# A hybrid attention/SSD layer: TensorE's first phase put into program order, with the SSD blocks cut into two stages and the norms moved

## The chip, the core and the metric

The kernel runs on one core of a Trainium2 chip. The metric is the device time of one execution in microseconds (us), as the median of several runs; less is better. TensorE (PE in the profile) does the matmuls and the transposes and writes to PSUM; PEld is its weight load. VectorE (DVE), ScalarE (ACT) and GpSimd (POOL) work on the results, and SyncE (SP) issues the DMAs.

## What is computed

One layer of a streaming encoder over 2048 prompt tokens and 32 sample tokens, width 1024. The part that the change touches is the input projection and the SSD (Mamba-2) half of the mixer; the stick-breaking attention of the first token block runs beside it.

```python
h = rmsnorm(x, g_mix_pre)
proj = h @ w_in                     # q, k, v (512 each), z (512), xbc (768), dt (8)
xbc = silu(causal_conv4(xbc)); xh, bm, cm = split(xbc)
dt = softplus(dt_raw + dt_bias); a = -exp(a_log)
acum = cumsum(dt * a)               # in chunks
y = ((cm @ bm.T) * tril(exp(acum_t - acum_s))) @ (dt * xh)    # within a chunk
y += (cm * exp(acum)) @ h_in                                   # from the state before it
h_out = exp(acum_end) * h_in + (bm * exp(acum_end - acum) * dt).T @ xh
y = rmsnorm((y + d_skip * xh) * silu(z), g_ssm_out)
attn = stick_breaking(q, k, v)      # past keys and values come from a cache for the sample tokens
out = concat([rmsnorm(attn, g_attn_out), y]) @ w_out
# then residual, gated conv FFN, residual
```

## The kernel before

Tokens lie in four blocks (`SBS`): block 0 has 512 prompt and the 32 sample tokens, blocks 1 to 3 have 512 each. The kernel has a first phase (`phase_in`), which makes all projections and the SSD part of the four blocks, and then a tail in which the attention of block s+1 is interleaved with the output projection and the FFN of block s.

**Products.** A product is a 128-column piece of `w_in` times the block's tokens: `dense` (L118) issues three fp32r matmuls for each of eight 128-row pieces (weights and activations are split into a high and a low part), so 24 matmuls of 512 columns in blocks 1 to 3, and two tiles of 24 matmuls of 272 columns in block 0. All of them have line L126. A block has 22 products: six for the convolution (`wbx`, of which numbers 4 and 5 are B and C), four each for k, v, z and q. A product leaves PSUM from one of two banks named `o`, multiplied by `r`, the broadcast reciprocal root of the input norm (`kf` L293, or `t` L305 in the convolution). `weight` makes a weight's two parts: a DMA, a cast on ACT (L110) and a subtraction on POOL (L111); three weights are held.

**Block of tokens s, in the order in which the program writes it.** `take` splits x into `xhi` (ACT L262) and `xlo` (DVE L263); for block 0 it also sums the squares (POOL L242) and makes `r`. Then the six convolution products with their convolution and SiLU; the `dt` product (L333 to L336) and its chain of small operations (L344 to L387); then the SSD sub-blocks of 128 tokens (five in block 0, four in the others), each followed by one k product; the squares of the next block's x (`ahead`); four v products, each followed by transposes into a PSUM bank named `st` and a copy on ACT (L427, L429); four z products (the gate) with the sums of squares; the gated norm's `rstd_narrow`; four q products; and last the normed y, stored by DMA.

**An SSD sub-block** (`ssd_block`, L469) loads `acB` and `eA`, the broadcast cumulative sums, by DMA (L478, L484), subtracts and exponentiates (DVE L488, ACT L492, L493), multiplies C by B and by the state into PSUM bank `y` (L498, L500), masks (DVE L506), multiplies into `acB` (L510) and `eA` (L514), transposes x and B (L521, L532) and makes `xdt`, `xw` and `bT` from them (L523, L528, L534), does the products with `acB` (L538), and updates the state (L550 to L562). `st` is one PSUM bank, `y` another tile with one buffer; each of the tiles of `sd` (`acB`, `eA`, `xdt`, `xw`, `bT`) has one buffer.

**The norms' roots** (`rstd_steps`) are matmuls against ones into `st` (L154), two small DVE operations, a power on POOL (L172), and matmuls that broadcast the result, again into `st` (L183), which ACT copies out.

**Who sets the order.** The instruction order of every engine, TensorE too, is set at compile time by a list scheduler that runs a timeline of its own: of the instructions that it takes to be ready it picks the one written first. `pin` and `mark` add order edges between matmuls; before the change the first phase has them only in the attention's slots, and the products there are not pinned. In the tail all products are pinned.

**Early attention.** `early` is a generator: first the sample tokens' attention (`sample`), then the 32 slots of block 0's attention (`slots(0, 0)`: scores L769 and L773, weights L619 to L627, transposes L790, values L805). `build` advances it by `RATE` = 0.66 of a step after each of `phase_in`'s yields, from block 1 on.

```python
            for n in phase_in(kn, c2):
                debt += n
                while debt >= 1:
                    debt -= 1
                    next(early, None)
            for _ in early:
                pass
```

## Time and profile before

| | us |
|---|---|
| median of 3 runs | 3098.43 (3097.11 to 3099.04) |
| the profiled execution | 3091.8 |
| its span, first to last instruction | 3090.0 |
| PE busy / DVE busy / POOL busy / ACT busy in the span | 2881.3 / 1616.4 / 1297.2 / 1278.7 |
| mean granted TensorE clock | 0.970 of full speed |

The first phase ends in the profile at about 858 us, where the first operation of the tail (ACT L713) starts. A row of the windows view gives a stretch of time, its length, the busy time of PE, PEld, DVE, ACT and POOL with the number of instructions, then the granted TensorE clock, the DMA engines' share and GB/s. A row of the waits view gives who waited for which writer, the time in total, how often, and the longest. A row of the groups gives line, engine, operation, shapes and count, then busy time and the mean of one in ns, then idle time before them and what ended it. Busy times of a group count overlapping instructions once.

### The profile page before, as it was taken

How to read it: one execution, taken by the hardware profiler on the slowest of the kernel's cores; microseconds unless marked ns; L12 is line 12 of the kernel's file. 1: busy time of each engine (PE TensorE's matmuls, PEld its weight loads, DVE VectorE, ACT ScalarE, POOL GpSimd, SP SyncE). 2: the span in 40 equal slices, each digit the busy share in tenths (PEclk: the TensorE clock that was granted, in tenths of full speed). 3: DMA queues.
4: the chain of work that ended last, by engine and by line, in shares of the span. 5: the costliest groups of instructions: out<-in, count | busy, mean ns of one | idle time of the engine just before them, and what ended most of it. 6: DMA issues, size and time to landing. Idle time of an engine off the chain costs nothing.

```text
span 3090.0 us, 43496 instructions
## 1 busy us (share of the span) xinstructions
PE 2881.3 (93%) x16142; PEld 2340.0 (76%) x16142; DVE 1616.4 (52%) x2456; ACT 1278.7 (41%) x2511; POOL 1297.2 (42%) x1099
## 2 busy tenths in 40 slices
PE   7899899898898999999999999999999999999996
PEld 6786576676686989998767777785677778878885
DVE  5647757676537565433763434447544453443334
ACT  4325446644457654333653323347333343421211
POOL 4445456464456555554652222246322223521113
PEclk8989999899999999999999999999999999999998
DMA  3536755655574767776646554664554545665555
GB/s 101 179 116 214 249 178 182 195 171 154 164 278 150 234 213 254 234 263 244 220 151 201 179 176 164 208 228 151 192 175 159 178 167 205 191 211 197 176 195 175
DMA packets 242437, 592.57 MB, mean 192 GB/s; under 512 B 49514, under 2 KB 105650, under 8 KB 212658
## 3 DMA queue, kind: packets, MB, share of 16 engines
q1 hardware_dynamic: 242226, 589.78, 57.9%
q8 instruction: 129, 2.11, 0.3%
q14 instruction: 82, 0.67, 0.1%
HBM read 456.19 MB, written 133.50 MB: 191 GB/s over the span
## 4 chain that ended last, share of the span: by engine, by line
PE 67%; DVE 12%; DMA 7%; issue 5%; ACT 4%; POOL 4%; SPq 1%; DVEq 0%; POOLq 0%; ACTq 0%
PE o L126 37%; PE t L126 9%; PE u L126 9%; PE pa L805 4%; PE z L769 3%; PE pt L790 3%; DVE prow L622 2%; DMA acB<-acD 1%; DVE xcA L312 1%; POOL w L111 1%; DVE acB L488 1%; DMA xr<-xT 1%; DVE f L1040 1%; DMA t<-xT 1%; ACT w L110 1%
## 5 line engine op out<-in xcount | busy, mean ns | idle before, releaser
L126 PE MATMUL o<-xhi,w 128*128 128x512 f32 (+2 forms) x4640 | 1202.2, 343 | 33.4 <-DVE kf L293 11.1
L126 PEld LDWEIGHTS o<-xhi,w 128*128 128x128 f32 x4640 | 810.9, 192 | 146.6 <-DVE kf L293 12.6
L126 PE MATMUL o<-xlo,w 128*128 128x272 f32 (+2 forms) x2320 | 794.9, 343 | 13.5 <-DVE xlo L263 7.2
L111 POOL TENSOR_TENSOR w<-wraw,w 128x1024 fp32r<-128x1024 f32 (+2 forms) x172 | 396.7, 2307 | 291.1 <-ACT w L110 266.3
L126 PEld LDWEIGHTS o<-xlo,w 128*128 128x128 f32 x2320 | 444.3, 192 | 67.1 <-DVE xlo L263 9.5
L627 POOL TENSOR_TENSOR beta<-beta,prow 128x512 f32<-128x512 f32 (+4 forms) x264 | 265.3, 1006 | 449.8 <-DVE prow L622 409.8
L126 PE MATMUL o<-ah,w 128*128 128x272 f32 (+1 forms) x1344 | 362.0, 344 | 10.6 <-DVE f L1019 6.7
L972 POOL TENSOR_TENSOR y<-y,gb 128x512 f32<-128x512 f32 (+1 forms) x88 | 115.7, 1315 | 530.7 <-ACT gb L971 530.2
L622 DVE TENSOR_TENSOR_SCAN prow<-gam,prow,z 128x513 f32<-128x513 f32 x200 | 254.7, 1276 | 122.5 <-ACT beta L620 117.0
L126 PE MATMUL u<-xhi,w 128*128 128x512 f32 (+1 forms) x1056 | 300.9, 362 | 0.6 <-ACT r L189 0.5
L126 PEld LDWEIGHTS o<-ah,w 128*128 128x128 f32 x1344 | 235.7, 189 | 42.1 <-DVE f L1019 8.5
L110 ACT CAST w<-wraw 128x1024 fp32r<-128x1024 f32 (+2 forms) x172 | 171.3, 997 | 168.7 <-PE o L126 123.1
L619 ACT ACTIVATE gam<-z 128x512 f32<-128x512 f32 (+3 forms) x330 | 178.6, 542 | 131.0 <-PE z L769 77.5
L126 PE MATMUL o<-al,w 128*128 128x272 f32 (+1 forms) x672 | 227.3, 338 | 0.0
L126 PEld LDWEIGHTS u<-xhi,w 128*128 128x128 f32 x1056 | 189.0, 188 | 38.5 <-issue 4.0
L964 DVE SCALAR_TENSOR_TENSOR y<-gb,cv,y 128x512 f32<-128x512 f32 (+1 forms) x176 | 167.2, 951 | 81.6 <-ACT y L962 78.5
L793 ACT COPY wt<-pt 128x512 f32<-128x512 f32 (+3 forms) x282 | 147.8, 533 | 136.9 <-PE pt L790 135.3
L126 PE MATMUL u<-xlo,w 128*128 128x512 f32 (+1 forms) x528 | 190.3, 360 | 0.0
L790 PE MATMUL pt<-ident,beta 128*128 128x128 f32 x1088 | 177.7, 280 | 8.6 <-POOL beta L627 6.0
L790 PEld LDWEIGHTS pt<-ident,beta 128*128 128x128 f32 x1088 | 131.5, 143 | 63.1 <-issue 22.6
L620 ACT ACTIVATE beta<-z 128x512 f32<-128x512 f32 (+3 forms) x330 | 178.6, 541 | 0.0
L1019 DVE TENSOR_TENSOR f<-o,f 128x272 f32<-128x272 f32 (+1 forms) x208 | 114.0, 550 | 114.3 <-PE o L126 112.2
(253 smaller groups left out, 4452.3 us busy)
## 6 DMA issues: line engine op xcount, KB each, us to landing
w<-wS_up SPq DMA_DIRECT2D x132, 1024.0 KB, 5.0
w<-wS_dn SPq DMA_DIRECT2D x72, 768.0 KB, 4.7
w<-wS_out SPq DMA_DIRECT2D x47, 1024.0 KB, 6.2
wS_up<-w SPq DMA_DIRECT2D x44, 1024.0 KB, 4.8
wraw<-wup SPq DMA_DIRECT2D x44, 512.0 KB, 5.7
k<-kS SPq DMA_DIRECT2D x80, 256.0 KB, 4.0
wS_dn<-w SPq DMA_DIRECT2D x24, 768.0 KB, 4.4
w<-wS_dn SPq DMA_DIRECT2D x32, 512.0 KB, 4.2
```

The source lines that it names most:

```text
L110: nc.scalar.copy(hi[:, :n, :], raw[:, :n, :])
L111: nc.gpsimd.tensor_tensor(lo[:, :n, :], raw[:, :n, :], hi[:, :n, :].bitcast(F32), op=ALU.subtract)
L126: mm = nc.tensor.matmul(ps[:, : c1 - c0], l[:, k, :], at(r, k0 + k)[:, c0:c1], start=first and i == 0 and k == 0, stop=last and i == 2 and ...
L619: nc.scalar.activation(g[:, c0:512], z, AF.Sigmoid, scale=-0.125)
L620: nc.scalar.activation(b[:, :n], z, AF.Sigmoid, scale=0.125)
L622: nc.vector.tensor_tensor_scan(back(pr), back(g), z[:, 0:1].to_broadcast([P, n + 1]), self.kn.ones[:, 0:1] if prev is None else prev, op0= ...
L627: eng.tensor_tensor(b[:, :n], b[:, :n], pr[:, c0 + 1 : 513], op=ALU.mult)
L790: mm = nc.tensor.transpose(t[:, P * j : P * j + P], w[:, P * j : P * j + P], kn.ident[:])
L793: copy(wt[:, : n // P, P * b : P * b + P], t[:, :n].rearrange("p (i q) -> p i q", q=P))
L805: nc.tensor.matmul(av[DH * (j % 2) : DH * (j % 2) + DH, c0:], v[:, j, :], wt[:, j, c0:], start=kc == s and j < 2, stop=kc == 0 and j > 1,)
L964: nc.vector.scalar_tensor_tensor(y[:, :W], gb[:, i : i + W], kn.col(wc + i), y[:, :W], op0=ALU.mult, op1=ALU.add)
L972: nc.gpsimd.tensor_tensor(y[:, :W], y[:, :W], t, op=ALU.mult)
```

## The change

All matmuls and transposes are issued through a small class, `Ordered`. In the first phase it is strict: each one is pinned behind the one before, so TensorE runs the first phase in the order in which the program writes it. The program is rewritten to fit this.

Work is laid on 23 units to each block of tokens, which are 22 products and the `dt` product. `after(n, fn)` puts a function off by n units, and `todo` lists what is done after a unit. Blocks 1 to 3 take the `dt` product first, then convolution, k, v, q, and z last; block 0 takes `dt` as the fourth unit.

- The first three convolution products of block 0 leave PSUM by a plain ACT copy (`bare`); the factor `r`, the convolution and the SiLU follow when `r` is there. `r`'s two steps come after the second and the third unit.
- The chain behind `dt` is cut into four steps, after units 1, 4, 6 (block 0: 4, 7, 8).
- `ssd_block` becomes a generator with three parts: the loads and exponentials; a first stage with the transposes and the products of C; a second stage with the products with `acB` and the state. The stages come after units 8, 9, 10, 12, 13, 15, 16, 18 (block 0: 9 to 18). The loads of a sub-block follow the second stage of the one before it.
- The transposes of B go into the bank of `y`; the state's matmuls go ahead of the products with `acB`; the four DVE operations of L542 move to the first stage.
- The transposes of v come two units after their product. The next block's squares are spread over units 9 to 12, its `r` over the next two.
- The gated norm's two steps come three and four units after the last z product, which is in the next block of tokens; the normed y follows there.
- In `sample` the products with the values come one step later, and two yields are added at its end (12 yields where there were 10).

```diff
+class Ordered:
+    def __init__(self, kn):
+        self.kn, self.strict = kn, False
...
+    def put(self, mm):
+        if self.strict:
+            self.kn.pin(mm)
+            self.kn.mark(mm)
+        return mm
...
+    def root(s, sq, first, second, done=None):
+        r = rp.tile([P, 544], F32, name=f"r{s % 2}")
+        g = kn.rstd_steps(rp, psm, "st", [sq], SBS[s][1], D, out=r)
+        after(first, lambda: next(g))
+        after(second, lambda: (next(g), done and done()))
+        return r
+
+    def after(units, fn):
+        pend.append([units, fn])
+
+    def tick():
+        for p in pend:
+            p[0] -= 1
+        due = [p for p in pend if p[0] <= 0]
+        pend[:] = [p for p in pend if p[0] > 0]
+        for p in due:
+            p[1]()
...
+            bare = s == 0 and c in (4, 5, 0)
...
+                    if bare:
+                        nc.scalar.copy(raw[:, d0:d1], ps[:, p0:p1])
+                    else:
+                        nc.vector.tensor_tensor(raw[:, d0:d1], ps[:, p0:p1], r[:, c0 + p0 : c0 + p1], op=ALU.mult)
...
+        def block(b, stage):
+            def go():
+                next(small["blocks"][b], None)
+                if stage == 1 and b < nb - 1:
+                    next(small["blocks"][b + 1])
...
+            after(2, turn)
...
+            if c == 3:
+                rg = rp.tile([P, 544], F32, name=f"r{s % 2}")
+                g = kn.rstd_steps(rp, psm, "st", [small["sq"]], nt, 512, out=rg)
+                after(3, lambda: next(g))
+                after(4, lambda end=normed: (next(g), end(rg, xcA)))
...
+        dt_at = 3 if s == 0 else 0
+        units = cs[:dt_at] + [lambda: next(st)] + cs[dt_at:] + k + v + q + z
+        todo = {i: [lambda: next(st)] for i in ((4, 7, 8) if s == 0 else (1, 4, 6))}
+        for n, i in enumerate(range(9, 19) if s == 0 else (8, 9, 10, 12, 13, 15, 16, 18)):
+            todo.setdefault(i, []).append(block(n // 2, n % 2))
+        if not last:
+            for i in range(4):
+                todo.setdefault(9 + i, []).append(lambda i=i: ahead(i))
...
+            r = root(0, sq0, 2, 3, begin)
+        for i, unit in enumerate(units):
+            unit()
+            tick()
+            for f in todo.get(i, ()):
+                f()
+            yield 0.0 if s == 0 else RATE
+    while pend:
+        tick()
...
     nc.scalar.activation(eA[:, :, :q], eA[:, :, :q], AF.Exp)
+    yield
     h_in = hT[state["h"]] if hS is None else hS
+    ps = psm.tile([P, 512], F32, name="st")
+    for j in range(4):
+        kn.pe.transpose(ps[:q, j * P : j * P + P], xcA[:, j, sl], kn.ident[:])
     cy = psy.tile([P, 2, 512], F32, name="y")
+    kn.pe.transpose(cy[:q, 0, 3 * P : 4 * P], xcB[:, 0, sl], kn.ident[:])
...
+    for j in range(4):
+        nc.vector.scalar_tensor_tensor(
+            xcA[:, j, sl], xcA[:, j, sl], kn.col(C_DS + j), eA[:, j, :q], op0=ALU.mult, op1=ALU.add
+        )
+    yield
     ps = psm.tile([P, 512], F32, name="st")
+    for g in range(2):
+        kn.pe.matmul(
+            ps[g * 64 : g * 64 + 64, :256], bT[:q, g * 64 : g * 64 + 64],
+            xw[:q, 4 * g : 4 * g + 4, :].rearrange("p h d -> p (h d)"), start=True, stop=True,
+        )
     yt = psy.tile([P, 2, 512], F32, name="y")
...
+            kn.pe.strict = True
             early = chain(att.sample(c2), att.slots(0, 0))
...
             out = att.out
+            kn.pe.strict = False
```

More of the change, by code (lines that the diff above doesn't have):

```diff
@@ L266, in take @@
             )
-            if r is None:
+            if s == 0:
                 square(sq, x, k == 0)
-        return (xhi, xlo), r or root(s, sq)
+        return (xhi, xlo), sq
     wfirst = kn.weight(wp, a["wbx"][4])
@@ L294, in leave, with conv @@
             return dst
[L296 to L298 removed]
+        def conv(c):
             raw = tmp.tile([P, 550], F32, name="t")
@@ L330, in phase_in @@
-        for c0, c1 in tiles_of(nt):
-            ps = psd.tile([P, 512], F32, name="o")
-            for k in range(KC):
-                nc.tensor.matmul(
-                    ps[:16, : c1 - c0], wdt[:, k, :], xhi[k][:, c0:c1], start=k == 0, stop=False, skip_group_check=True
-                )
-                nc.tensor.matmul(
-                    ps[:8, : c1 - c0], wdt[:, k, 0:8], xlo[k][:, c0:c1], start=False, stop=k == KC - 1,
-                    skip_group_check=True,
-                )
-            nc.vector.tensor_tensor(dtr[:16, c0:c1], ps[:16, : c1 - c0], r[:16, c0:c1], op=ALU.mult)
@@ L444, in phase_in, with gate @@
+        def gate(c):
+            z = leave(a["wz"][c])
+            xcA = xc["A"]
             t = tmp.tile([P, 550], F32, name="t")
@@ new lines, in ahead @@
+        def ahead(i):
+            nonlocal nxt
+            if i == 0:
+                small["sqn"] = tmp.tile([P, 544], F32, name="sq", bufs=1)
+            for k in (2 * i, 2 * i + 1):
+                square(small["sqn"], load(s + 1, k), k == 0)
+            if i == 3:
+                nxt = root(s + 1, small["sqn"], 1, 2)
+        q, k, v, z = (
+            [(lambda c=c, f=f: f(c)) for c in range(4)]
+            for f in (lambda c: keys("wq", kn.qS, c), lambda c: keys("wk", kn.kS, c), val, gate)
+        )
@@ L647, in sample, with values @@
         av = self.pa.tile([P, 512], F32, name="pa", bufs=1)
-        prev = [None, None]
+        prev, late = [None, None], []
+        def values():
+            for kc, g, q, nsub, wt, v in late:
+                for i in range(nsub):
+                    for e in range(2):
+                        kn.pe.matmul(
+                            av[DH * e : DH * e + DH, P * g : P * g + P], wt[:q, P * i + DH * e : P * i + DH * e + DH],
+                            v[:q, i, P * e : P * e + P],
+                            start=kc == 4 and g == 0, stop=kc == 0 and g == 1 and i == 3, skip_group_check=True,
+                        )
+            late.clear()
         for kc in (4, 3, 2, 1, 0):
```

430 lines of the change are left out of this document (224 added, 206 removed).

## The prediction

> **What bounds the kernel now.** I read the page first.
>
> ```profile
> span 3090.0 us, 43496 instructions
> PE 2881.3 (93%) x16142; PEld 2340.0 (76%) x16142; DVE 1616.4 (52%) x2456; ACT 1278.7 (41%) x2511; POOL 1297.2 (42%) x1099
> ```
>
> PE is busy for 93% of the span and no other engine for more than 52%, so PE's path sets the time, and a change can win only where PE is idle or its clock is held down. The windows view, cut at the starts of the four token blocks and at the end of the first phase (858 us), says where that is.
>
> ```profile
> 0.00:40.00 40.00, 17.78 (x80) 15.98 (x81) 19.71 (x28) 17.52 (x28) 24.44 (x30) 0.74 0.41 142
> 40.00:236.00 196.00, 172.79 (x1290) 161.46 (x1289) 107.34 (x229) 65.74 (x106) 80.25 (x48) 0.90 0.43 132
> 236.00:450.00 214.00, 190.50 (x987) 139.06 (x985) 144.15 (x215) 100.89 (x155) 113.46 (x67) 0.95 0.65 209
> 450.00:655.00 205.00, 185.00 (x902) 138.02 (x901) 143.22 (x211) 117.30 (x188) 113.23 (x77) 0.93 0.61 191
> 655.00:858.00 203.00, 180.42 (x876) 133.66 (x877) 128.70 (x204) 93.82 (x157) 98.49 (x67) 0.95 0.54 171
> 858.00:3090.00 2232.00, 2134.80 (x12018) 1751.84 (x12014) 1073.27 (x1573) 883.45 (x1882) 867.37 (x811) 0.99 0.59 198
> ```
>
> In the first phase PE is busy for 746.5 of 858 us, which leaves 111.5 us idle, at a clock of 0.74 to 0.95. The tail, whose products are pinned, is busy for 2134.8 of 2232 us (96%) at 0.99. So more than half of PE's whole idle time of 208.7 us lies in 28% of the span, and it is the part that the change rewrites. Next, the same view for the stretches in which the small slices dip, and one without a dip for comparison.
>
> ```profile
> 24.00:37.00 13.00, 4.51 (x20) 3.96 (x20) 0.45 (x3) 1.63 (x2) 6.17 (x5) 0.50 0.19 68
> 100.00:120.00 20.00, 14.77 (x100) 13.08 (x99) 13.57 (x24) 5.54 (x8) 12.16 (x9) 0.83 0.68 218
> 140.00:180.00 40.00, 29.23 (x182) 24.96 (x183) 19.34 (x61) 7.19 (x13) 5.41 (x4) 0.66 0.30 90
> 285.00:400.00 115.00, 94.11 (x550) 66.35 (x550) 78.64 (x140) 58.07 (x84) 58.07 (x38) 0.91 0.71 236
> 485.00:600.00 115.00, 98.22 (x507) 70.50 (x506) 82.70 (x150) 74.78 (x114) 61.95 (x45) 0.90 0.66 207
> 680.00:790.00 110.00, 94.84 (x470) 67.73 (x468) 77.09 (x148) 51.63 (x79) 44.14 (x27) 0.91 0.44 137
> 400.00:440.00 40.00, 39.98 (x180) 32.47 (x181) 20.03 (x24) 13.32 (x19) 22.18 (x13) 1.00 0.45 132
> ```
>
> And the windows view of the products alone (L126):
>
> ```profile
> 180.00:230.00 50.00, 47.70 (x369) 1.00 0.45 134
> 370.00:400.00 30.00, 2.90 (x13) 0.77 0.58 193
> 580.00:600.00 20.00, 0.00 (x0) 0.66 0.45 143
> 770.00:790.00 20.00, 0.00 (x0) 0.74 0.38 120
> 400.00:440.00 40.00, 38.94 (x163) 1.00 0.45 132
> ```
>
> The pattern is the same in every token block. While SSD sub-blocks run, products are used up as filler, and at the end of the SSD stretch none is left: 370 to 400, 580 to 600 and 770 to 790 hold 2.9 us of products in 70 us. Small matmuls then wait for one another there, and the clock drops to 0.66 to 0.77. After it the remaining products run back to back at full clock. The waits view of PE in 0 to 860 us names the waits:
>
> ```profile
> PE y L538 <- DVE acB L510: 12.2, 10, 2.4
> PE o L126 <- DVE kf L293: 11.1, 6, 5.2
> PE z L769 <- DVE prow L622: 10.7, 12, 2.0
> PE o L126 <- DVE xlo L263: 7.2, 5, 4.4
> PE o L126 <- ACT xhi L262: 6.9, 1, 6.9
> PE st L154 <- POOL sq L242: 6.2, 1, 6.2
> PE st L550 <- ACT bT L534: 5.7, 4, 2.2
> ...
> PE st L183 <- ACT r L181: 0.7, 1, 0.7
> ```
>
> These are many short waits of a chain on itself (the longest 6.9 us), not one late engine.
>
> **The change part by part.** It adds and removes hardly any work on PE. What it moves is when products stand between the links of the chains. I take each stretch's idle time and its clock loss as what can be won, and then a share. Clock loss is bounded by busy time times (1 minus the clock): at most that if all of it is limited by the array, nothing if it is waiting time.
>
> *The start (bare copies).* The timeline of PE:
>
> ```profile
> 23.73 0.43 PE L126 MATMUL o<-xhi,w 128*128 128x272 f32 x1
> 30.41 2.06 PE L154 MATMUL st<-ones,sq 128*128 128x1 f32 x10 [6.25 <-POOL sq L242]
> ...
> 37.26 0.59 PE L126 MATMUL o<-xhi,w 128*128 128x272 f32 x1
> ```
>
> The first product ends at 24.2 us and fills both `o` banks, which cannot be emptied before `r` exists, so the next product starts at 37.26. With plain copies out, two products fit there: 48 matmuls at 47.70/369 = 0.129 us are 6.2 us each. Their weights are there in time: by POOL's timeline the third weight of the phase ends at 22.3:
>
> ```profile
> 19.41 2.84 POOL L111 TENSOR_TENSOR w<-wraw,w 128x1024 fp32r<-128x1024 f32 x1
> ```
>
> The root's matmuls (4.51 us at half clock) are still to be done, about half of that at full clock: 13 - 2.3 = 10.7, taken as **-11**. The 13.7 us idle in the first 40 us outside this stretch are x arriving and being split; they stay.
>
> *The `dt` chain and the SSD of block 0* (100 to 120 and 140 to 180). Idle 5.2 + 10.8 = 16.0; clock at most 14.77 x 0.17 + 29.23 x 0.34 = 12.4; together 28.4. The chain's steps now have a product or more between them. The tight place is a sub-block's loads, which go out behind the second stage of the one before, two products (12.4 us) ahead of its own second stage. These rows are of DVE's waits and groups:
>
> ```profile
> DVE acB L488 <- DMA acB<-acD: 40.2, 12, 7.3
> ```
>
> ```profile
> L488 DVE TENSOR_SCALAR acB<-acB,acum 128x128 f32<-128x128 f32 (+1 forms) x136 | 43.0, 387 | 40.4 <-DMA acB<-acD 40.2
> L446 DVE TENSOR_TENSOR t<-kf,t 128x512 f32<-128x512 f32 (+1 forms) x16 | 37.7, 2359 | 19.6 <-ACT t L445 19.6
> L510 DVE TENSOR_TENSOR acB<-acB,cbm 128x512 f32<-128x512 f32 (+1 forms) x34 | 30.1, 925 | 6.8 <-ACT acB L492 6.8
> ```
>
> Load at its longest 7.3, eight L488 at 0.387 are 3.1, two L510 at 0.925 are 1.9: 12.3 us before the exponential is counted. That is no margin, so I take three quarters: **-21**.
>
> *The SSD stretches of blocks 1 to 3.* Idle 20.9 + 16.8 + 15.2 = 52.9; clock at most 94.11 x 0.09 + 98.22 x 0.10 + 94.84 x 0.09 = 26.8; together 79.7. Here three products lie between a load and its second stage, 3 x 24 x 38.94/163 us = 17.2 against the 12.3, and first and second stage stand one or two products (5.7 or 11.5 us) apart. DVE is busy for 0.68 to 0.72 of these stretches, so it can keep up but will at times be late with emptying an `o` bank (the 11.1 us of kf waits). I take 0.7: **-56**. The bounds are 0 and 79.7.
>
> How much of it is clock? The row of 580 to 600 has a clock of 0.66, and the longest PE wait listed between 578 and 602 is 2.2 us:
>
> ```profile
> PE st L550 <- ACT bT L534: 2.2, 1, 2.2
> ```
>
> So here the clock fell without a long gap, in a stretch of small matmuls only, and products set between them should hold it at 1.00 as in 400 to 440. The Trainium skill, TensorE: Matmul & The Clock Gate, section "HAM oscillation — how this bites in real kernels", gives the abstract rule of no PE-idle gaps above about 3.4 us; this stretch disagrees with it as the sole condition. By that rule no wait that I expect behind the change would cost clock, and the 39.2 us of clock bounds above would come back whole instead of at three quarters and 0.7: about 11 us more.
>
> *New: `st` changes hands with nothing between.* In program order a v transpose, a root step and a stage of a sub-block follow one another after units 12 to 15, all through the one bank `st`, and PE, now strictly in order, stands until ACT or DVE has emptied it; behind it the next product waits. By the lists I count six such places in block 0, five each in blocks 1 and 2, three in block 3: 19. The nearest row is the same kind of handover, L183 behind ACT's copy, 0.7 us; the upper is the bT wait, 5.7/4 = 1.4. 13 to 27; I take the nearest: **+13**.
>
> *New: z is last.* In blocks 0 to 2 the gated norm's first matmuls come a product and the `dt` product later, which covers the chain. After block 3 nothing is left but the end of the early attention, so PE stands for the gate's chain, in which L446 alone is 2.4 us; q's products did cover that. Between nothing and twice to three times this: **+5**. The same order takes q's stores off the end, off PE's path.
>
> *At nothing:* more exponential/sigmoid alternation on ACT and three more DVE operations, under 144 of 214 us DVE busy at most; the moved DMAs on SP, as long as three weights are ahead.
>
> Sum: -11 - 21 - 56 + 13 + 5 = **-70 us**. The profiled execution took 3091.8 us with a span of 3090.0, which would become 3020; the median of the runs is 3098.43 (3097.11 to 3099.04), so the forecast is **3028 us**.
>
> **The rivals.**
>
> *All of it comes back.* The stages are far enough apart, nothing waits and the clock stays at 1.00: -11 - 28 - 80 + 9 for handovers and end (half of the 18) is -110, 2988 us. For it: 400 to 440 and the pinned tail. Against it: DVE at 0.7. The clock rule cited above would work this way. Chance 0.17.
>
> *Waits move.* Each of the 34 stages waits as the bT reader does now, 1.4 us: 48 us, so -22, 3076 us. For it: PE can no longer take a product while a link is late, and an attention step (z behind prow, 12 waits now) sits in the same line. Against it: the spacing. Chance 0.15, of which 0.04 is no change.
>
> *Slower.* The loads of `acB` sit in SP's queue behind stores and weights that wait, and every second stage waits for them; in order, nothing can pass. At the longest load wait of today, 7.3 us, 17 sub-blocks give +124 and with the -70 a time of 3152. It decides from 70/17 = 4.1 us each. For it: this is DVE's second largest wait (40.2 us). Against it: today it is paid with one product between sub-blocks, not two or three. Chance 0.12.
>
> That the order is not really changed I leave out: the pins reach every matmul of the phase.
>
> **How the numbers follow.** Forecast, -35 to -95 us: 0.56. A measurement tells about 0.2% (6 us) from no change. Faster by more: 0.56 + 0.17 + 0.11 = 0.84; within: 0.04; slower: 0.12. The range is 2980 to 3095: it leaves out the slower case, the no-change part and the far end of the full gain, 0.2 in all.
>
> **What would show it.** Right: the first phase ends near 788 us; products start again right behind 24 us; clock 0.97 or more from 50 us on; no stretch of 20 us without products; L538 and L550 almost gone from PE's waits; `st` readers behind ACT copies with about 20 waits of 0.7 us. Wrong: PE waits of over 3 us at L538 behind acB, DVE above 0.85 in the SSD stretches, or waits of L126 behind L293 grown past 11 us. The tail should be the same to within a few us; a gain or a loss there would be a cause that I have not seen.

## The result and the profile after

| | before | after |
|---|---|---|
| median of 4 runs, us | 3097.77 (3094.78 to 3099.04) | 3136.05 (3130.27 to 3141.71) |
| the profiled execution's span, us | 3090.0 | 3133.6 |
| its granted TensorE clock | 0.970 | 0.962 |
| end of the last projection product, us | 839.8 | 859.1 |
| PE idle up to there, us | 106.5 | 137.1 |

The change makes the kernel slower: ratio 1.0125, 95% interval [1.0105, 1.0145], 38 us. The forecast was 70 us faster. (Of the four runs of f5_noload, further down, one took 4339.69 us at a granted clock of 0.591 for 0.976 to 0.979 in the others; its ratio is of those three.)

The first two lines of the page after:

```profile
span 3133.6 us, 43470 instructions
...
PE 2888.5 (92%) x16142; PEld 2352.5 (75%) x16142; DVE 1612.0 (51%) x2453; ACT 1297.6 (41%) x2534; POOL 1300.4 (41%) x1099
```

The work is the same; PE is busy for 7 us more and idle for 36 us more. Where the idle time lies is read from the windows view. First each kernel from its start to the end of its last projection product; before:

```profile
0.00:839.80 839.80, 733.26 (x4055) 579.79 (x4056) 532.70 (x869) 382.42 (x601) 416.61 (x274) 0.92 0.55 172
```

and after:

```profile
0.00:859.10 859.10, 722.03 (x4017) 577.13 (x4018) 517.45 (x858) 398.20 (x617) 417.24 (x271) 0.92 0.54 169
```

PE's idle time is the second number less the third: 106.5 and 137.1 us. The clock over the whole stretch is the same 0.92 (a better start makes up for 0.92 instead of 0.94 from 50 us on), so it is mainly idle time that was added. Of the 43.6 us by which the span grew, 19.3 are there by the last product, 10.9 lie between it and the 100th matmul of the tail's products, and 13.4 in the rest of the tail.

Now the stretches of the prediction, after:

```profile
24.00:37.00 13.00, 12.92 (x85) 12.89 (x85) 1.32 (x3) 3.75 (x9) 4.96 (x3) 0.79 0.15 51
...
140.00:180.00 40.00, 31.34 (x231) 28.69 (x228) 13.71 (x43) 8.90 (x14) 7.87 (x5) 0.88 0.35 112
285.00:400.00 115.00, 98.09 (x551) 73.14 (x551) 65.58 (x101) 59.80 (x84) 63.53 (x37) 0.94 0.77 254
485.00:600.00 115.00, 94.26 (x449) 71.52 (x448) 75.87 (x121) 68.05 (x101) 64.59 (x41) 0.90 0.66 215
680.00:790.00 110.00, 89.56 (x442) 70.50 (x440) 73.82 (x126) 53.49 (x83) 50.77 (x30) 0.91 0.50 155
```

And products alone (L71 into `o`, which includes the `dt` product):

```profile
580.00:600.00 20.00, 11.26 (x43) 0.91 0.76 239
770.00:790.00 20.00, 9.49 (x40) 0.93 0.50 158
```

The change does what it says. The start is filled (4.51 us busy became 12.92), products now stand in the stretches that had none, and there the clock is 0.91 to 0.93 where it was 0.66 to 0.74 (370 to 400, with 12.79 us of products for 2.90, has 0.89 for 0.77). But the SSD stretches as wholes are hardly fuller: 98.09 for 94.11, 94.26 for 98.22, 89.56 for 94.84. The gaps are now between the products instead of behind them. PE's waits in 0 to 890 us, after:

```profile
PE o L71 <- DVE xlo L293: 19.8, 12, 6.8
PE st L71 <- ACT khi L474: 17.7, 8, 5.7
PE o L71 <- ACT xhi L292: 14.4, 4, 6.5
PE st L74 <- DVE xcA L363: 13.4, 2, 7.9
PE z L71 <- DVE prow L735: 13.0, 6, 6.2
PE pa L71 <- ACT wt L803: 11.1, 4, 4.1
PE st L74 <- ACT khi L474: 10.6, 5, 3.3
PE st L71 <- ACT klo L483: 7.3, 3, 6.5
...
PE st L71 <- ACT r L201: 5.9, 2, 4.8
...
PE st L71 <- POOL sq L519: 4.6, 1, 4.6
PE y L71 <- DVE acB L637: 4.1, 1, 4.1
PE st L74 <- ACT r L209: 2.8, 3, 1.5
```

The waits that were the aim are gone: of the wait for L510's `acB` (12.2 us, ten times) one is left, L637, and the wait for `bT` is not listed. Longer ones came: for the copies of v's transposes out of `st` (khi, klo), for the roots' copies (r), for the last convolution's SiLU (xcA L363), for the early attention's own steps (prow, wt), and for x (xhi, xlo): 17.7 of these 34.2 us are block 0's x at the start, 16.5 the next block's x at a block's end.

What is late behind a 6 us wait? PE's timeline in block 0, then ACT's in the same stretch (start, duration, engine, line, operation, and in brackets the idle time before and who ended it):

```profile
130.69 0.60 PE L74 MATMUL st<-ident,kf 128*128 128x128 f32 x4
132.51 0.29 PE L74 MATMUL st<-ident,kf 128*32 128x128 f32 x1 [1.23 <-ACT khi L474]
139.33 1.12 PE L71 MATMUL st<-xw,bT 128*64 128x256 f32 x4 [6.53 <-ACT klo L483]
```

```profile
131.88 0.58 ACT L474 COPY khi<-st 128x512 f32<-128x512 f32 x1
138.41 0.63 ACT L604 ACTIVATE eA<-eA 128x512 f32<-128x512 f32 x1 [5.95 <-DMA eA<-acD]
138.94 0.24 ACT L483 COPY klo<-st 32x128 f32<-32x128 f32 x1
```

PE put a transpose into `st` at 132.51 and needs the bank back for the state's matmuls. The copy that empties it takes 0.24 us, but in ACT's queue it stands behind the exponential on `eA`, and ACT stood 5.95 us there for a DMA. SP issued that load at 134.62, since `eA` has one buffer, and its last reader (L647) had ended at 134.59:

```profile
134.62 1.29 SPq L595 DMA_DIRECT2D eA<-acD  x2
```

So PE stands for ACT, and ACT for a load; each runs its instructions in the order set for it.

This is the longest of the waits for khi and klo, and not all are of its kind. Eleven of them are over 1 us, 32.8 us together. In five (16.3 us) an exponential on `eA` or `acB` is one of the two instructions just ahead of the copy in ACT's queue; in the other six the one just ahead is a cast, of a weight (L130) or of k or q (L492).

### The profile page after: what moved, and what is told of

It reads as the page before. It is cut to its first block, busy times and chain, and to the rows that moved or that the text cites. A ratio compares the mean times of both kernels' runs of the same rounds, so it can differ in the third digit from the quotient of the medians.

```text
span 3133.6 us, 43470 instructions
## 1 busy us (share of the span) xinstructions
PE 2888.5 (92%) x16142; PEld 2352.5 (75%) x16142; DVE 1612.0 (51%) x2453; ACT 1297.6 (41%) x2534; POOL 1300.4 (41%) x1099
## 4 chain that ended last, share of the span: by engine, by line
PE 71%; DVE 8%; DMA 6%; ACT 4%; issue 3%; POOL 2%; SPq 1%; ACTq 0%; DVEq 0%; POOLq 0%
PE o L71 40%; PE u L71 9%; PE t L71 9%; PE pa L71 4%; PE z L71 4%; PE pt L74 3%; DVE prow L735 2%; DMA xr<-xT 1%; PE y L71 1%; DMA eA<-acD 1%; DMA xr<-hS 1%; ACT w L130 1%; DMA acB<-acD 1%; DVE f L1166 1%; PE st L71 1%
## 5 line engine op out<-in xcount | busy, mean ns | idle before, releaser
L71 PE MATMUL o<-xhi,w 128*128 128x512 f32 (+2 forms) x4640 | 1209.8, 344 | 27.8 <-ACT xhi L292 6.5
L71 PEld LDWEIGHTS o<-xhi,w 128*128 128x128 f32 x4640 | 818.3, 193 | 142.5 <-issue 13.4
L71 PE MATMUL o<-xlo,w 128*128 128x272 f32 (+2 forms) x2320 | 796.0, 343 | 18.8 <-DVE xlo L293 11.2
L71 PEld LDWEIGHTS o<-xlo,w 128*128 128x128 f32 x2320 | 447.5, 193 | 67.9 <-DVE xlo L293 12.6
L71 PE MATMUL o<-ah,w 128*128 128x272 f32 (+1 forms) x1344 | 362.5, 345 | 9.8 <-DVE f L1145 7.3
L71 PE MATMUL u<-xhi,w 128*128 128x512 f32 (+1 forms) x1056 | 300.8, 362 | 0.6 <-ACT r L209 0.5
L130 ACT CAST w<-wraw 128x1024 fp32r<-128x1024 f32 (+2 forms) x172 | 171.3, 996 | 252.1 <-PE o L71 185.3
L71 PEld LDWEIGHTS o<-ah,w 128*128 128x128 f32 x1344 | 236.4, 189 | 41.4 <-DVE f L1145 9.9
L71 PE MATMUL o<-al,w 128*128 128x272 f32 (+1 forms) x672 | 227.9, 339 | 0.0
L71 PEld LDWEIGHTS u<-xhi,w 128*128 128x128 f32 x1056 | 188.9, 188 | 38.5 <-issue 4.0
L71 PE MATMUL u<-xlo,w 128*128 128x512 f32 (+1 forms) x528 | 190.3, 360 | 0.0
L74 PE MATMUL pt<-ident,beta 128*128 128x128 f32 (+1 forms) x1122 | 183.4, 281 | 4.8 <-POOL beta L740 3.6
L74 PEld LDWEIGHTS pt<-ident,beta 128*128 128x128 f32 (+1 forms) x1122 | 135.3, 143 | 60.3 <-issue 26.0
```

The source lines that it names most:

```text
L71: return self.put(self.kn.nc.tensor.matmul(*args, **kw))
L74: return self.put(self.kn.nc.tensor.transpose(*args, **kw))
L130: nc.scalar.copy(hi[:, :n, :], raw[:, :n, :])
```

## The experiments

The reading of the trace gave this theory: program order on PE is itself the cost, since PE then inherits every late place in ACT's and DVE's queues; among these the loads of `acB` and `eA` are the largest, and the block's edges are the next. The rivals: the one bank `st`; the lateness of one engine (ACT); the new places themselves, whatever the order. All ratios are to the kernel before, timed beside each kernel on the same chip; brackets are 95% intervals. Differences from the changed kernel are differences of ratios times 3098 us, a few us off from the differences of the medians. Idle is PE's idle time up to the last projection product, from rows as above. The last two columns are of one profiled execution each: f1_zq's and f4_zqeexp's are the longest of their four, p4_attfree's and q1_eexp's the shortest.

| kernel | median, us | ratio | last product, us | PE idle to there, us |
|---|---|---|---|---|
| before | 3097.77 | 1 | 839.8 | 106.5 |
| after | 3136.05 | 1.0125 [1.0105, 1.0145] | 859.1 | 137.1 |
| x1_free | 3077.95 | 0.9937 [0.9922, 0.9952] | 807.0 | 88.9 |
| x2_oldpin | 3271.34 | 1.0567 [1.0549, 1.0584] | 993.6 | 241.4 |
| x3_vbank | 3133.48 | 1.0122 [1.0102, 1.0141] | 854.2 | 139.6 |
| x4_end | 3129.01 | 1.0105 [1.0082, 1.0128] | 858.0 | 136.2 |
| p1_rate | 3142.85 | 1.0156 [1.0131, 1.0180] | 877.5 | 143.8 |
| p2_vfree | 3138.40 | 1.0132 [1.0106, 1.0158] | 864.8 | 142.0 |
| p3_zq | 3117.22 | 1.0076 [1.0045, 1.0106] | 856.5 | 134.2 |
| p4_attfree | 3116.76 | 1.0068 [1.0046, 1.0091] | 842.6 | 120.7 |
| q1_eexp | 3123.66 | 1.0078 [1.0054, 1.0103] | 843.8 | 129.3 |
| q2_vdve | 3133.33 | 1.0112 [1.0082, 1.0142] | 854.8 | 133.2 |
| r1_noload | 3104.63 | 1.0017 [1.0004, 1.0030] | 831.9 | 121.5 |
| r2_sum | 3103.61 | 1.0019 [1.0006, 1.0033] | 832.8 | 117.0 |
| f1_zq | 3058.47 | 0.9870 [0.9850, 0.9890] | 792.4 | 77.9 |
| f4_zqeexp | 3065.16 | 0.9898 [0.9878, 0.9918] | 798.1 | 81.6 |
| f5_noload | 3048.18 | 0.9822 [0.9792, 0.9852] | 780.9 | 76.9 |

### The order, with and without the new places

x1_free keeps every new place and takes the pins away:

```diff
-            kn.pe.strict = True
+            kn.pe.strict = False
```

> The changed program with the strict order of TensorE switched off in the first phase, so that the scheduler again chooses the order; spacing, z last and everything else as changed. Theory A (TensorE in order stands behind late releases, above all of the one bank st: 52.8 us of its 144.8 us of waits in the changed first phase): 3070 to 3105 us, 30 to 65 us under the changed kernel's 3136, and the waits of st readers behind ACT copies fall from 52.8 us to under 20. Rival B (the moves cost, not the pinning: z last and dt first at a block's edge, the late start, the end): 3125 us or more, with the same waits at the edges.

x2_oldpin is the kernel before, untouched but for the class `Ordered` and `strict = True` over its first phase: the pins without the new places.

> The kernel before with one thing added: all matmuls and transposes of the first phase pinned in program order; no step is moved. Theory A: much slower than before, since each SSD sub-block's chain then stands on TensorE's path with one product between: by 17 sub-blocks at 8 to 12 us each, 3230 to 3300 us. Rival B: pinning costs little, under 3130 us.

The four combinations are: old places free 3098, old places pinned 3271, new places free 3078, new places pinned 3136. The pins cost 173 us on the old places and 58 on the new. The new places are worth 20 us without pins and 135 with them. PE's waits of x1_free:

```profile
PE z L71 <- DVE prow L735: 15.6, 11, 3.2
PE o L71 <- DVE xlo L293: 9.9, 4, 6.7
PE o L71 <- ACT xhi L292: 9.4, 3, 6.7
PE o L71 <- DVE t L343: 8.6, 3, 4.4
```

No `st` reader is among the first; those behind ACT's copies, 44.6 us in the changed kernel (the expectation's 52.8 counts other readers of `st` too), are down to 4.3. The waits for x at the blocks' ends fell from 16.5 to 4.4 us: the scheduler has put other matmuls ahead of what is late. And of the old places with pins:

```profile
PE st L74 <- DVE xdt L543: 40.9, 17, 7.7
PE y L71 <- DVE acB L530: 38.3, 28, 7.0
```

Here the chain of every sub-block shows on PE (17 times `xdt`, 28 times `acB`). The new places do take these away; they were made for the pins, and make good most of what the pins cost.

### The bank, and the engine that empties it

x3_vbank puts v's transposes into the attention's bank `pt`:

```diff
-                ps = psm.tile([P, 512], F32, name="st")
+                ps = kn.ptv.tile([P, 512], F32, name="pt")
```

> The changed kernel with the transposes of v written to the early attention's bank pt instead of st. Theory A: the 36 us of waits behind the copies of v (khi, klo) shrink to 10 to 15, some come back as waits for pt; 3105 to 3122 us, 14 to 30 us under the changed kernel. Rival B: within 6 us of 3136.

The ratio is that of the changed kernel. The wait changed its bank and kept its releaser:

```profile
PE pt L74 <- ACT khi L474: 28.9, 8, 8.1
```

Not the bank, then: the copy of khi is late wherever it copies from. p2_vfree leaves only v's transposes out of the strict order:

```diff
             def turn(s=s):
+                kn.pe.strict = False
...
+                kn.pe.strict = True
```

> The changed kernel with only the transposes of v taken out of the strict order; everything else stays pinned. Theory A (a pinned TensorE stands in front of the next reader of st until ACT has copied v out): 3100 to 3116 us, and the waits of st behind khi and klo fall from 35.9 us to under 12. Rival B (ACT is late anyway, so the stages of the SSD behind them wait for the same copy wherever the transposes stand): 3125 or more.

No gain, as the rival said: the stage behind waits for the same copies (khi 14.0 and 10.5 us, klo 8.0). q2_vdve moves the copies from ACT to DVE:

```diff
-                nc.scalar.copy(vt[:, :512], ps[:])
+                nc.vector.tensor_copy(vt[:, :512], ps[:])
```

> The changed kernel with the copies of v's transposes out of PSUM on VectorE in place of ScalarE; order as in the changed kernel. Theory (they are late since ScalarE stands ahead of them): TensorE's waits for v's copies (khi 17.7 and klo 7.3 us, and 10.6 us of transposes behind them) fall to a third and the time is 3112 to 3128. Rival (VectorE's queue is as late at these places, behind the normed rows and the SSD's multiplies): 3130 or more.

3133.33, 1.0112 [1.0082, 1.0142]: no difference that can be told from the changed kernel. The waits for khi are nearly as long, behind the other engine (klo's 7.3 us fell to 1.3):

```profile
PE st L71 <- DVE khi L474: 16.7, 8, 4.9
...
PE st L74 <- DVE khi L474: 10.9, 5, 5.2
```

The theory that ACT alone is late fell here. One thing that DVE stands for itself is `acB`'s load; in the changed kernel and then in q2_vdve:

```profile
DVE acB L599 <- DMA acB<-acD: 33.4, 14, 6.3
```

```profile
DVE acB L599 <- DMA acB<-acD: 41.1, 14, 5.6
```

DVE's subtraction stands for `acB`'s load, as ACT's exponential stands for `eA`'s. That this is what makes the copies late on DVE was not tested by itself; the next two runs take the loads' waits away.

### The loads

q1_eexp takes exp(acum) once for a block, stores it, and loads `eA` already exponentiated, so ACT no longer touches `eA`:

```diff
+            exT = so.tile([P, 544], F32, name="khi")
+            nc.scalar.activation(exT[:n8, :P], ps[:n8, :P], AF.Exp)
+            nc.sync.dma_start(kn.acE[s][:n8, :], exT[:n8, :P])
...
-    nc.scalar.activation(eA[:, :, :q], eA[:, :, :q], AF.Exp)
```

> The changed kernel with exp(acum) taken once for the whole block and stored, so that the eA tiles of the SSD stages are loaded already exponentiated and ScalarE's 17 exponentials on eA are gone; order as in the changed kernel. Theory (ScalarE's own queue stands at exponentials whose loads are late, the copies and casts behind it are late, and TensorE in program order stands for them): ScalarE's idle time ahead of the eA exponentials, 54.6 us in the changed kernel, is gone, the waits for the copies behind them shrink, and the time is 3110 to 3125. Rival (the exponential on acB stands for its own load in the same place and takes the wait over): 3130 or more.

3123.66, within the theory's bounds; by the ratios 15 us less than the changed kernel. ACT's idle time at `eA` is gone, but a part of it came back at `acB`, as the rival had it, and the waits for khi did not shrink (17.8 + 14.6 us for 17.7 + 10.6; klo's fell from 7.3 to 1.2). ACT's waits, q1_eexp:

```profile
ACT L606 <- DVE acB L602: 35.0, 4, 10.6
ACT acB L606 <- DVE acB L602: 34.4, 9, 8.3
```

That is 69.4 us where the changed kernel has 35.4 + 19.3 = 54.7. (An ACT wait without a tile is a table load, 1.28 us in these traces, ahead of the operation.) r1_noload leaves out both loads in all but the first sub-block of a block and keeps every instruction; what it computes is no longer the layer, so it prices the loads and is no kernel to use:

```diff
+    if b == 0:
+        acB = sd.tile([P, 8, P], F32, name="acB")
...
+        kn.kept["ab"] = acB, eA
+    acB, eA = kn.kept["ab"]
...
-    nc.scalar.activation(eA[:, :, :q], eA[:, :, :q], AF.Exp)
+    nc.scalar.activation(eA[:, :, :q], eA[:, :, :q], AF.Exp, scale=0.0)
```

> The changed kernel, which leaves out the loads of acB and eA in all but the first of a block's SSD blocks (the later ones work on what the tiles hold; the exponential on eA with a scale of nought, so that numbers stay finite): every instruction of VectorE and ScalarE is kept, only what they stand for is gone. Theory (the loads, late since each tile has one buffer, hold VectorE's subtraction and ScalarE's exponentials, and all that is queued behind them): VectorE's wait for acB (33.4 us) and ScalarE's for eA (54.6) go, those of ScalarE's exponential for the subtraction shrink to half or less, TensorE's listed waits fall by 25 us or more, and the time is 3095 to 3115. Rival (the waits that TensorE stands for come from the order of the queues, whichever instruction stands first; with the loads gone the next late instruction takes their place): 3122 or more.

3104.63, 1.0017 [1.0004, 1.0030]: 33 us less than the changed kernel, as the theory said. The mechanism came out only in half. DVE's wait for the load fell from 33.4 to 3.6 us, but ACT's waits at these places mostly changed their cause:

```profile
ACT acB L606 <- DVE acB L602: 39.9, 11, 5.7
...
ACT eA L607 <- DVE xcA L650: 24.8, 7, 5.8
...
ACT L607 <- DVE xcA L650: 16.9, 5, 6.6
```

ACT now waits for the last reader of the one buffer (L650 here, L647 in the changed kernel, where it is what lets the load start) instead of for the load behind it. PE's listed waits in 0 to 890 us fell from 144.8 to 132.4 us, half of the 25 expected. Its idle time to the last product fell by 15.6 us, and its busy time by 11.6 us (710.40 for 722.03) at a clock of 0.94 for 0.92:

```profile
0.00:831.90 831.90, 710.40 (x4017) 570.14 (x4018) 522.28 (x858) 404.34 (x621) 418.50 (x271) 0.94 0.52 163
```

So the loads, their lateness and their traffic together, are worth some 33 us of the time in program order. Of the waits for v's copies they account for about 13 of 35.6 us: khi still has 15.1 + 6.2 for 17.7 + 10.6, klo 1.2 for 7.3. Nine of the remaining ones are over 1 us, and in each of them the cast of a weight (L130) is among the two instructions just ahead of the copy; what those casts cost was not tested. A second buffer for both tiles, which would take away the lateness and leave the traffic, was not run.

### The edges, the end and the early attention

x4_end lets the early attention run out before the last norm, which is left unpinned:

```diff
+    yield 99.0
+    kn.pe.strict = False
     while pend:
```

> The changed kernel with its end altered: the early attention is run out before the last block's gated norm, and that norm's matmuls are not pinned. The time between the last product of the first phase and the first product of the tail was 4.6 us before and is 19.3 us in the changed kernel. Theory A (the last norm stands in TensorE's line): that gap falls to 6 to 9 us, 3122 to 3127 us. Rival B (the rest of the attention is the bound there): under 4 us gained.

1.0105 for 1.0125, 6 us by the ratios, but the intervals overlap. The way into the tail fell from 18.7 to 14.4 us (from the last product's end to the tail's first product, 1.8 before; the expectation counted otherwise), not to the 6 to 9 expected, so neither reading is shown. p1_rate spreads the early attention faster:

```diff
-RATE = 0.66
+RATE = 0.75
```

> The changed kernel with RATE 0.75 instead of 0.66, so that the early attention, which has two more yields than before, is through several products before the end of the first phase. Theory A (the late attention lengthens the way into the tail: its eighth head is copied out at 875 us, 16 us behind the last product, where before it was 51 us ahead of it): 3120 to 3128 us. Rival B (the way into the tail is set by other things): within 4 us of 3136.

No gain (1.0156); the wait of z behind prow grew from 13.0 to 18.4 us. p4_attfree instead lets it out of the line; all else stays pinned:

```diff
+                    kn.pe.strict, held = False, kn.anchor
                     next(early, None)
+                    kn.pe.strict, kn.anchor = True, held
```

> The changed kernel with only the early attention taken out of the strict order; products, SSD, norms and v transposes stay pinned among themselves. Theory A (each link in TensorE's line that waits for ACT or DVE costs; the attention's are z behind prow 13.0, values behind wt 11.8, att_s 1.4 us): 3108 to 3122 us. Rival B (the attention's steps wait in slack that products would not have filled): 3130 or more.

1.0068: 18 us back, 16.5 of them before the last product. p3_zq puts z's products ahead of the last three of q's in blocks 1 to 3, so that the gate's chain is over by the block's end:

```diff
-        units = cs[:dt_at] + [lambda: next(st)] + cs[dt_at:] + k + v + q + z
+        units = cs[:dt_at] + [lambda: next(st)] + cs[dt_at:] + k + v + (q + z if s == 0 else q[:1] + z + q[1:])
-        for n, i in enumerate(range(9, 19) if s == 0 else (8, 9, 10, 12, 13, 15, 16, 18)):
+        for n, i in enumerate(range(9, 19) if s == 0 else range(8, 16)):
```

> The changed kernel with, in blocks 1 to 3, z ahead of the last three q products, and the SSD stages after units 8 to 15 instead of 8 to 18. Block 0 as changed. Theory A (z last holds up the splitting of the next block's x and, in block 3, the way into the tail): the waits for xhi and xlo after 400 us fall from 11 us to under 5 and the 6 us at the last norm go, 3110 to 3122 us; closer stages may cost 5 to 10 of it. Rival B (closer stages lose more than the edges win): 3136 or more.

1.0076: 15 us back, but not where I looked for it. In the profile the last product ends 2.6 us earlier and the tail's first product follows after 9.5 us instead of 18.7, yet by the 100th matmul of the tail's products only 0.5 us of that is left. Nearly the whole gain lies in the rest of the tail, whose time varies between kernels (below). So neither the end nor the inner edges are shown to be better (12.3, 5.2 and 16.7 us from the last product to the first convolution product of the next block, for 12.5, 13.0 and 14.7).

r2_sum is p3_zq, p4_attfree and q1_eexp in one, pinned.

> The changed kernel, in program order, with three edits together that gave 20, 19 and 11 us alone: the early attention out of the order, z ahead of the last three of q's with the SSD stages over units 8 to 15, and exp(acum) once for a block. Theory (each edit takes away waits at its own places): they add up to some 45 to 50 us, 3085 to 3095, level with the kernel before. Rival (they take away the same waits, or one edit's place is another's cover): 3105 or more.

1.0019 [1.0006, 1.0033]: 33 us of the 15 + 18 + 15 = 48 that the parts gave alone, between theory and rival. Whether they overlap is not shown: up to the 100th matmul of the tail's products the parts gave 0.5, 14.2 and 13.0 us in their profiles, 27.8 in sum, and the three together 23.6; most of what is missing is p3_zq's gain in the tail. With three edits the pinned kernel comes level with the kernel before, not ahead of it.

### The best order

f1_zq is x1_free with p3_zq's places, f4_zqeexp is f1_zq with q1_eexp's exponential, and f5_noload is f1_zq without the loads, as in r1_noload.

> The order left to the dependences (strict order off, spacing and places as in the changed kernel), and in blocks 1 to 3 z's three products ahead of the last three of q's, with the SSD stages over units 8 to 15. Theory (the waits for the previous block's norm at the block's end stay whatever the order, and q's products are better cover for them than z's): 10 to 20 us below the same kernel without the move (3077.95), 3055 to 3070. Rival (with the order free the scheduler fills those places already): 3073 or more.

> The same as the kernel with the order left free and z ahead of the last three of q's, with exp(acum) taken once for a block and stored as well. Theory (ScalarE's standing at late loads costs in the free order too, but less, since other products fill in): 5 to 15 us below that kernel, 3045 to 3065. Rival (in the free order ScalarE's wait is wholly hidden): the same as that kernel within 4 us.

> The order left free, z ahead of the last three of q's, and the loads of acB and eA left out as in the other kernel without them. Theory (in the free order other products fill in while the loads are late, so they cost little): 3050 to 3060, within 8 us of the same kernel with its loads (3058.47). Rival (the late loads cost in the free order as well): 3045 or less.

f1_zq takes 3058.47 us, 0.9870 [0.9850, 0.9890]: faster than the kernel before by 40 us, than x1_free by 21 by the ratios, and than the changed kernel by 79. f4_zqeexp gives nothing more (0.9898, 7 to 9 us slower if anything, where the rival had the same within 4), so with the order free taking the exponential off `eA` gains nothing. f5_noload at 3048.18 falls between its two expectations: the loads cost 10 to 15 us in the free order, against 33 pinned. Its ratio's interval touches that of f1_zq, but each of the three runs behind it is below each of f1_zq's four. In the profiles PE's idle time is the same (76.9 for 77.9) and the clock is higher:

```profile
0.00:780.90 780.90, 704.05 (x4025) 565.05 (x4026) 540.69 (x861) 387.65 (x610) 416.14 (x272) 0.96 0.54 173
```

for f1_zq's row:

```profile
0.00:792.40 792.40, 714.51 (x4025) 572.93 (x4026) 527.89 (x861) 396.27 (x616) 413.95 (x272) 0.94 0.57 182
```

## Why the prediction was wrong

**What bounds the kernel: right.** The idle time to be won lay in the first phase, and PE's path set the time. The four combinations show that it can move by 190 us and more.

**The start, -11: right.** The second product ends 10.2 us earlier. The first ends 5.8 us later (30.0 for 24.2): in order, its second tile waits until the first tile has its last piece of x, where the free order let both follow x as it came. That was not in the sum.

**Block 0, -21, and the SSD stretches, -56: the first failed step.** From the second product to the end of block 0 the changed kernel loses 7 us instead of gaining 21, and from there to the last product it loses 23 instead of gaining 56. Less the growth of the block edges, +39 us in sum, the blocks 1 to 3 gain some 16, of which some 11 are the three `dt` products that moved into the edges. I took shares of what could be won as if the spacing alone decided, and put program order down as the means to it. It was a cost of its own, for which the sum had no term but the +13 for `st`. Part by part, in the profiles:

| stretch, us | forecast | before | after | x1_free (no pins) |
|---|---|---|---|---|
| start to the end of the second product | -11 | 46.2 | 36.0 | 33.9 |
| from there to block 0's last product | -21 | 189.9 | 196.7 | 172.9 |
| from there to the last product (blocks 1 to 3) | -56 | 603.7 | 626.4 | 600.2 |
| from there to the 100th matmul of the tail's products | +5 | 35.3 | 46.2 | 49.9 |
| the rest of the tail | 0 | 2214.9 | 2228.3 | 2216.1 |

(The +13 for `st` belongs to the second and third rows together. The cuts are at products, so SSD work may cross them.) Without pins the start and block 0 gain 12.3 and 17.0 us, near the forecast; the blocks 1 to 3 gain 3.5 of 56. So the pins cost 24 us in block 0 and 26 in blocks 1 to 3, and the share of 0.7 that I took for blocks 1 to 3 was too large even without them. Why so little comes back there stays open: without pins PE is idle in them for 60.6 us, before for 61.1, both at a clock of 0.94.

The argument for the pins was the tail, pinned and 96% busy. It does not carry over; as I read it, because the stages of the first phase hang on chains through ACT and DVE with single-buffered loads in them.

**`st` changes hands, +13: mechanism right, size wrong by a factor of three.** I expected about 20 waits of 0.7 us. The `st` readers behind ACT's copies (khi twice, klo, and r twice in the list above) are 8 + 5 + 3 + 2 + 3 = 21 waits and 17.7 + 10.6 + 7.3 + 5.9 + 2.8 = 44.3 us, 2.1 each. The row that I took, a root's copy of 0.7 us, was of a copy with nothing late ahead of it: ACT had been idle for 10.90 us when it came. The price of a handover in order is set by what stands ahead of the copy. For khi neither the bank nor the engine matters (x3_vbank, q2_vdve).

**z last, +5 and the edges covered: the second failed step.** At the end the norm's two waits, 4.64 for `sq` and 1.35 for `rn_v`, make 6.0, near the +5:

```profile
864.05 1.87 PE L71 MATMUL st<-ones,sq 128*128 128x1 f32 x8 [4.64 <-POOL sq L519]
867.27 2.07 PE L71 MATMUL st<-ident,rn_v 128*128 128x128 f32 x8 [1.35 <-POOL rn_v L192]
```

But from the last product to the tail's first there are 18.7 us for 1.8, since the early attention comes to its end there too: its eighth head is copied out some 16 us behind the last product, where before that was some 51 us ahead of it. And the edges of blocks 0 to 2, which I had put at nothing, are the larger price: 12.5, 13.0 and 14.7 us from a block's last product to the next convolution product, for -0.1, 0.3 and 0.6. Take the last of them, PE after:

```profile
655.79 0.39 PE L71 MATMUL o<-xhi,w 128*128 128x512 f32 x1
...
659.54 0.41 PE L71 MATMUL o<-xhi,wdt 128*16 128x512 f32 x1 [2.60 <-ACT xhi L292]
661.52 0.59 PE L71 MATMUL o<-xlo,wdt 128*8 128x512 f32 x1 [1.58 <-DVE xlo L293]
...
670.91 0.48 PE L71 MATMUL o<-xhi,w 128*128 128x512 f32 x1
```

What I had called cover, the `dt` product, stands there for the next block's x, and uses up the pieces faster than a product does (two matmuls to each piece instead of three). ACT's queue in the same place has gate and casts in one line, the casts each behind an x load:

```profile
658.22 0.65 ACT L508 ACTIVATE t<-kf 128x512 f32<-128x512 f32 x1
658.75 1.34 ACT L292 ACTIVATE xhi<-t,cv 128x512 fp32r<-128x512 f32 x2
660.35 1.39 ACT L292 ACTIVATE xhi<-t,cv 128x512 fp32r<-128x512 f32 x2 [0.26 <-DMA t<-xT]
662.10 0.63 ACT L518 ACTIVATE t<-xcA 128x512 f32<-128x512 f32 x1 [0.37 <-DVE xcA L510]
...
664.73 0.72 ACT L292 ACTIVATE xhi<-t,cv 128x512 fp32r<-128x512 f32 x1 [1.37 <-DMA t<-xT]
```

I had listed the gate's chain as something that the next block covers, and not that the next block's x goes through the same queue. A part of each edge is the `dt` product itself, which only moved: sixteen matmuls, 3.8 us at the prediction's 38.94/163 = 0.239 us. In the edge shown they start 0.43 us apart, at a granted clock of 0.64 (659.5 to 669.0 us). In the free order the same edges are 6.4, 5.4 and 4.1: 24 us of the three go with the pins.

**The clock.** In the places that had no products it rose from 0.66 to 0.74 to 0.91 to 0.93, short of the 1.00 that I took from 400 to 440. From 50 us on to the last product it is 0.92; I had asked for 0.97, and the kernel before has 0.94. The Trainium skill, TensorE: Matmul & The Clock Gate, section "HAM oscillation — how this bites in real kernels", has the rule of no gaps above about 3.4 us that the prediction weighed. Behind the second product PE now stands for more than 3.4 us at a time ten times (54.3 us in all), where it did so twice (9.5 us). The lower clock goes that way, the stretch of 580 to 600 before went against it, and no run here tells long gaps from stretches of small matmuls.

**Put at nothing: ACT's exponentials and sigmoids in turn.** Up to the last product ACT's table loads rose from 50 to 64, of 1.28 us each. r1_noload has 68 and is 33 us faster, so they do not decide; what the 14 cost was not measured.

**The tail, "the same to within a few us": not settled.** Behind the 100th matmul of its products it takes 2228.3 us for 2214.9, and 11.6 of these 13.4 us are PE's busy time, at a clock of 0.98 for 0.99. Among the kernels here, whose tail is written the same, that part takes from 2211.1 (p3_zq) to 2229.3 us (x3_vbank) in their single profiles, with PE idle for 91 to 101 us in each. What sets the clock there I did not find; the runs of one kernel differ by as much (q2_vdve 3121.44 to 3142.10).

**The rivals.** "Slower" had the right resource, the loads of `acB` and `eA`, and the right reason, that in order nothing can pass. Its place was wrong: it looked for the wait at L538, where 4.1 us are listed, while what shows of it stands at the copies behind ACT's exponentials; and r1_noload prices it at 33 us, or 2.5 for each of 13 sub-blocks, not 7.3 for each of 17. "Waits move" had 48 us of waits, near the 44.3 found by luck (34 of 1.4 us were counted, 21 of 2.1 came), but kept the gains beside them. What I left out of both is that the price of order and the gain of spacing are not two sums that can be added.

## What to carry to other kernels

Before an engine is put into program order, price the order by itself: each place at which it waits for another engine costs what stands ahead in that engine's queue, loads included, and not the bare copy; and try the new places with the order left free as well. Where a wait follows the copy to another bank and another engine, read what stands ahead of the copy in each queue, and price that: here the loads were a third of it, not the whole. An operation that begins the next block is no cover for the end of the last, when its inputs go through the same queue.

## What was not expected of the hardware

Taking loads away raised the granted clock beside shortening the waits. In program order it is 0.94 for 0.92 up to the last product, and 0.966 to 0.973 over r1_noload's ten whole runs for 0.962 to 0.966 over the changed kernel's four. In the free order the profiles have 0.96 for 0.94, with PE's idle time the same within 1 us and its busy time down by 10.5 us; but the profile of f1_zq is the longest of its four runs, and the whole runs differ less (0.976 to 0.979 over three for 0.969 to 0.976 over four). Whether fewer DMAs or another mix of matmuls did that, the runs don't tell.
